# Retention's values and gate projected together by seven half-size products, in a single-core hybrid decoder block

## The chip, the core and the metric

The kernel runs on one core of a Trainium2 chip. A core has five engines with queues of their own, each worked through in order: TensorE (PE: matmuls, and PEld, its weight loads), VectorE (DVE), ScalarE (ACT), GpSimd (POOL) and SyncE (SP, which here only issues DMAs). The metric is device time in microseconds (us), the median of several executions; less is better.

## The reference

One decoder layer on 512 tokens of 1024 features, float32. What matters here is its front:

```python
h = rmsnorm(x, g_mix[l])
z = h @ w_in[l]
q_r, k_r, v_r, gt_r, q_f, k_f, v_f, f_f, a_r, a_f = split_cols(z)
q_r = rotary(...); k_r = rotary(...) * (RET_DK ** -0.5)
o_r = retention_chunkwise(q_r, k_r, v_r)        # 4 heads, values of 128, chunks of 128
...                                             # group norm of o_r
y_r = (silu(gt_r) * o_r) @ w_ret_o[l]
...                                             # forgetting attention of q_f, k_f, v_f: 8 heads of 64
x = x + (sigmoid(a_r) * y_r + sigmoid(a_f) * y_f) @ w_out[l]
x = x + swiglu(rmsnorm(x, g_ffn[l]))
```

v_r (values) and gt_r (gate) have 512 columns each and stand side by side in w_in: together a product of 512 x 1024 by 1024 x 1024. The norm's factor 1/rms of each token (rstd1) is applied after the products, since it is one number per token.

## The kernel before

Every float32 factor is split in a high and a low part (xh, xl of x times g_mix; wh, wl of weights), and a product is three matmuls: high by high, low by high, high by low (`three`). A weight unit is 128 x 1024 (0.5 MB): `load_w` issues its DMA on SP into one of two raw tiles, `split_raw` makes wh on ACT (a cast, L152) and wl on DVE (a subtraction, L153) in one of three pairs of tiles (WB = 3), used in turn. A pair is written again when PE has done with it, a raw tile when wl is made.

The order of the work: first the columns of retention's q and k (8 feature blocks by 4 token blocks, 96 matmuls into PSUM banks sc and tp), with loads and splits of x and weights running just ahead. Beside it x comes again, token by token; ACT squares and sums it (L220) and DVE makes rstd1 by a shift and three Newton steps (`rsqrt`, 12 instructions on 128x4). ACT then copies the four banks to rz, times rstd1.

Then the values: `tok_group`, 96 matmuls with 512 columns into the four acc banks, each copied by ACT to vr times rstd1. Then a stretch whose PE order is written out by hand (`pinned`): retention for four token blocks (rotation on POOL, `ret_rotate`; transposes, scores, states, norm, output) and the attention (`fox_scores`, `fox_turn`, `fox_values`, a chain of 32 steps), with a filling between their parts. `Fill` holds generators of independent matmuls and gives out so many us of them, by a cost of its own, at each call: the gate (group 4, with silu), the attention's q, k and v, and two of four pairs of gate tiles (`gates(mp)`, the columns a_r and a_f). RF, CF, PF and SF are the shares given out at each place; `fill.until(n)` empties all but n generators. Behind the attention the rest of the block follows: the third and fourth pair of gate tiles with the output projections, w_out, and the feed-forward part, which already computes its products by seven half-size products each.

Elsewhere the order on an engine is a scheduler's: it places instructions by its own estimate of when they are ready, and `after(a, b)` keeps a behind b.

Of the kernel before, what the change touches and what calls it, by code (L numbers as in the profile page):

```python
# [17 lines left out]
P = 128  # L18
# [34 lines left out]
@with_exitstack  # L53
def block_kernel(ctx: ExitStack, tc, x, xT, c_early, c_tab, c_late, w_qf, w_tok, w_a, w_y, w_o, w_gu, w_dn, w_dh, out):
    nc = tc.nc
# [53 lines left out]
    def rsqrt(dst, ss, inv_n, shape, nm, pool=None, behind=None):  # L109

        v = (pool or sm).tile(shape, F32, name=nm + "v", tag=nm + "v", bufs=1 if pool else 2)
        yi = (pool or sm).tile(shape, I32, name=nm + "y", tag=nm + "y", bufs=1 if pool else 2)
        a = (pool or sm).tile(shape, F32, name=nm + "a", tag=nm + "a", bufs=1 if pool else 2)
        y = yi.bitcast(F32)
        first = ts(out=v, in0=ss, scalar1=inv_n, scalar2=EPS, op0=ALU.mult, op1=ALU.add)
        if behind is not None:
            after(first, behind)
        ts(out=yi, in0=v.bitcast(I32), scalar1=1, scalar2=None, op0=ALU.logical_shift_right)
        ts(out=yi, in0=yi, scalar1=-1.0, scalar2=float(0x5F3759DF), op0=ALU.mult, op1=ALU.add)
        for i in range(3):  # L120
            stt(out=a, in0=y, scalar=-0.5, in1=y, op0=ALU.mult, op1=ALU.mult)
            tt(out=a, in0=a, in1=v, op=ALU.mult)
            stt(out=dst if i == 2 else y, in0=a, scalar=1.5, in1=y, op0=ALU.add, op1=ALU.mult)

# [23 lines left out]
    def split_raw(raw, width=1024):  # L148
        pool, bufs = next_pool(part_pools, 1)
        h = pool.tile([P, WP if pool is wp else 1024], F32R, name="wh", tag="wh", bufs=bufs)  # L150
        l = pool.tile([P, WP if pool is wp else 1024], F32R, name="wl", tag="wl", bufs=bufs)
        nc.scalar.copy(out=h[:, :width], in_=raw[:, :width])  # L152
        tt(out=l[:, :width], in0=raw[:, :width], in1=f32(h)[:, :width], op=ALU.subtract)  # L153
        return h, l
# [59 lines left out]
    pinned[0] = False  # L214
    ahead = [load_w(w_tok[3, u]) for u in range(2)]
    for t2 in range(2):
        nc.sync.dma_start(out=xs[t2], in_=x[t2 * 256:(t2 + 1) * 256].rearrange("(t p) d -> p t d", p=P))
    for t in range(NT):
        junk = ftok.tile([P, D], BF16, name="junk", tag="sq", bufs=1)
        act(out=junk, in_=xs[t // 2][:, t % 2, :], func=AF.Square, accum_out=ss1[:, t:t + 1])  # L220
    rsqrt(rstd1, ss1, 1.0 / D, [P, NT], "n1")
    nc.sync.dma_start(out=ctab, in_=c_tab)

# [75 lines left out]
    for t in range(NT):
        evac_to(rz, AF.Copy)(t, 0, accs[t])  # L300

    def unit(group):
        return lambda u, width: w_tok[group, u]

    run(tok_group(unit(3), evac_to(vr, AF.Copy), ahead=ahead))
    broadcast_cols(rstd1, r1)
# [12 lines left out]
    def ret_rotate(t):  # L319
# [138 lines left out]
    def fox_prep(a, part):  # L458

        if part == 0:  # L460
# [5 lines left out]
            for e, (r, o) in enumerate(((ra, rb), (rb, ra))):  # L466
                act(out=tk[e][r], in_=pk[r], func=AF.Copy, scale=gk[r])  # L467
                act(out=tk[e][o], in_=pk[r], func=AF.Copy, scale=gk[r])  # L468
                stt(out=kl[e][r], in0=pk[r], scalar=gk[r], in1=f32(tk[e])[r], op0=ALU.mult, op1=ALU.subtract)  # L469
            fox["k", a] = tk, kl  # L470
        else:
# [107 lines left out]
    fill.until(3)  # L579
    rwk.release()  # L580
# [69 lines left out]
    for mp in range(4):  # L650
        if mp > 0:
            if mp == 1:
                fill.until(0)
            else:
# [4 lines left out]
        for m2 in range(2):  # L659
# [346 lines left out]
def _layout(i):  # L1006
# [18 lines left out]
    def halves(m):  # L1025
# [42 lines left out]
```

## Time and profile before

| | us |
|---|---|
| median of 3 runs (715.22 to 717.8) | 716.05 |
| profiled execution, device time | 717.38 |
| its span, first to last instruction | 715.6 |
| PE busy | 708.9 |
| DVE busy | 509.2 |
| ACT busy | 344.0 |
| POOL busy | 70.1 |

A row of a group names line, engine, operation, what it writes and reads, shapes and count; then busy us, mean ns of one; then the engine's idle time just ahead of it and what ended it. A row of the timeline begins with start and length in us. A row of busy time by stage gives the stretch, its length, then for PE, PEld, DVE, ACT and POOL the busy time and in brackets the number of instructions, then the granted clock, the DMA engines' share and GB/s. A row of the chain has start, length, and the instructions merged.

### The profile page before, as it was taken

Reading aid. Unit: us, or ns where it says so; the run is one execution under the profiler, and the core shown is the slowest. Engines: PE = TensorE matmul, PEld = TensorE weight load, DVE = VectorE, ACT = ScalarE, POOL = GpSimd, SP = SyncE. Lnnn points to the kernel's source line nnn. Section 1 sums busy time; section 2 is a strip of 40 time slices with the busy share of each in tenths; the row PEclk is TensorE's granted clock in tenths of the full one; section 3 lists DMA queues with packets and bytes.
Section 4 is the critical chain, followed back from the end, with each engine's and each line's share of the span. In section 5 each row is a group of like instructions: output and inputs, shape, how many; then the busy total and the mean of one; then the engine's idle time right before and its main releaser. Section 6 shows DMA issues by size and latency. Waiting matters only on the chain.

```text
span 715.6 us, 10855 instructions
## 1 busy us (share of the span) xinstructions
PE 708.9 (99%) x4307; PEld 623.7 (87%) x4307; DVE 509.2 (71%) x844; ACT 344.0 (48%) x532; POOL 70.1 (10%) x90
## 2 busy tenths in 40 slices
PE   8999999999999999999999999999999999999998
PEld 6888998888777688888888999999999998888998
DVE  6333667756878673545968798899888998854684
ACT  4542434446766732233654755655665555533251
POOL 0163502121311100000220000000000000000000
PEclk9999999999999999999999999999999999999999
DMA  8632222233212023326603233322332213353112
GB/s 286 248 118 90 63 87 62 87 121 119 96 65 73 31 89 101 105 89 220 221 1 117 69 110 119 118 71 106 120 118 92 86 56 122 120 173 99 56 69 75
DMA packets 19908, 76.34 MB, mean 107 GB/s; under 512 B 2312, under 2 KB 2952, under 8 KB 16656
## 3 DMA queue, kind: packets, MB, share of 16 engines
q1 hardware_dynamic: 19712, 75.62, 31.2%
q8 instruction: 34, 0.56, 0.3%
q14 instruction: 18, 0.15, 0.1%
q10 hardware_dynamic: 144, 0.02, 0.0%
HBM read 73.52 MB, written 2.11 MB: 106 GB/s over the span
## 4 chain that ended last, share of the span: by engine, by line
PE 92%; DVE 3%; ACT 2%; issue 1%; POOL 1%; DMA 1%; SPq 0%; DVEq 0%; ACTq 0%
PE acc L72 59%; PE sc L72 27%; PE tp L72 5%; PE tp L75 2%; DVE pr L499 1%; POOL cb L491 1%; DVE pr L503 1%; DMA raw<-in_w_tok_dram 1%; ACT pr L501 1%; ACT tk L468 0%; DVE tq L478 0%; ACT tk L467 0%; DVE kl L469 0%; DVE sg L548 0%; DVE ofl L172 0%
## 5 line engine op out<-in xcount | busy, mean ns | idle before, releaser
L152 ACT CAST wh<-raw 128x1024 fp32r<-128x1024 f32 (+1 forms) x52 | 54.5, 1050 | 123.4 <-PE acc L72 97.4
L153 DVE TENSOR_TENSOR wl<-raw,wh 128x1024 fp32r<-128x1024 f32 (+1 forms) x52 | 66.6, 1282 | 48.4 <-ACT wh L152 48.3
L72 PE MATMUL sc<-xfh,cl 128*128 128x256 f32 x288 | 83.2, 289 | 0.0
L72 PE MATMUL sc<-xfh,ch 128*128 128x256 f32 x288 | 81.6, 283 | 0.0
L72 PE MATMUL sc<-xfl,ch 128*128 128x256 f32 x288 | 81.4, 283 | 0.0
L72 PE MATMUL acc<-wh,xh 128*128 128x512 f32 (+2 forms) x192 | 69.7, 363 | 0.0
L741 DVE TENSOR_TENSOR cl<-t,ch 128x1024 fp32r<-128x1024 f32 x48 | 58.6, 1222 | 13.7 <-ACT ch L741 13.6
L72 PE MATMUL acc<-wh,xl 128*128 128x512 f32 (+2 forms) x192 | 68.2, 355 | 0.0
L72 PE MATMUL acc<-wl,xh 128*128 128x512 f32 (+2 forms) x192 | 68.0, 354 | 0.0
L72 PE MATMUL acc<-xfh,ah 128*128 128x256 f32 (+1 forms) x216 | 63.9, 296 | 0.0
L72 PE MATMUL acc<-xfh,al 128*128 128x256 f32 (+1 forms) x216 | 63.7, 295 | 0.0
L72 PE MATMUL acc<-xfl,ah 128*128 128x256 f32 (+1 forms) x216 | 63.7, 295 | 0.0
L741 ACT CAST ch<-t 128x1024 fp32r<-128x1024 f32 x48 | 50.5, 1052 | 12.8 <-PE tp L72 8.0
L72 PEld LDWEIGHTS sc<-xfh,cl 128*128 128x128 f32 x288 | 55.0, 191 | 0.8 <-DVE cl L741 0.2
L72 PEld LDWEIGHTS sc<-xfh,ch 128*128 128x128 f32 x288 | 55.1, 191 | 0.1
L72 PEld LDWEIGHTS sc<-xfl,ch 128*128 128x128 f32 x288 | 55.1, 191 | 0.0
L72 PE MATMUL acc<-xh,wh 128*128 128x512 f32 x128 | 51.8, 404 | 0.0
L72 PE MATMUL acc<-xh,wl 128*128 128x512 f32 x128 | 50.0, 391 | 0.0
L72 PE MATMUL acc<-xl,wh 128*128 128x512 f32 x128 | 49.9, 390 | 0.0
L741 DVE TENSOR_TENSOR al<-raw,ah 128x1536 fp32r<-128x1536 f32 x24 | 42.2, 1757 | 6.9 <-ACT ah L741 6.9
L72 PEld LDWEIGHTS acc<-xfh,al 128*128 128x128 f32 x216 | 41.3, 191 | 1.0
L72 PEld LDWEIGHTS acc<-xfl,ah 128*128 128x128 f32 x216 | 41.3, 191 | 0.9
(294 smaller groups left out, 1796.3 us busy)
## 6 DMA issues: line engine op xcount, KB each, us to landing
raw<-in_w_gu_dram SPq DMA_DIRECT2D x21, 1024.0 KB, 4.8
raw<-in_w_tok_dram SPq DMA_DIRECT2D x16, 512.0 KB, 3.7
raw<-in_w_a_dram SPq DMA_DIRECT2D x16, 512.0 KB, 3.6
t<-in_w_dn_dram SPq DMA_DIRECT2D x14, 512.0 KB, 3.7
raw<-in_w_y_dram SPq DMA_DIRECT2D x8, 512.0 KB, 3.6
raw<-in_w_o_dram SPq DMA_DIRECT2D x8, 512.0 KB, 3.7
raw<-in_w_dh_dram SPq DMA_DIRECT2D x4, 1024.0 KB, 4.8
xf<-in_xT_dram SPq DMA_DIRECT2D x8, 256.0 KB, 5.0
```

The source lines that it names most:

```text
L72: in_order(nc.tensor.matmul(o, **kw))
L75: in_order(nc.tensor.transpose(out=o, in_=src, identity=ident))
L152: nc.scalar.copy(out=h[:, :width], in_=raw[:, :width])
L153: tt(out=l[:, :width], in0=raw[:, :width], in1=f32(h)[:, :width], op=ALU.subtract)
L491: gp.tensor_tensor(out=cb[:, qs], in0=cb[:, qs], in1=mask, op=ALU.add)
L499: nc.vector.tensor_tensor_reduce(out=pr[:, :n], in0=cb[:, :n], in1=sc[:, :n], scale=-1.0, scalar=3e38, op0=ALU.add, op1=ALU.min, accum_out=nm)
L501: fox["last"] = act(out=pr[:, :n], in_=pr[:, :n], func=AF.Exp, scale=-1.0, bias=nm, accum_out=rs)
L503: ts(out=pr[:, :n], in0=pr[:, :n], scalar1=ri, scalar2=None, op0=ALU.mult)
L741: split_to.last = nc.scalar.copy(out=h, in_=src), tt(out=l, in0=src, in1=f32(h), op=ALU.subtract)
```

## The change

Values and gate are computed as one product by a scheme with seven half-size products in place of eight. x's transposed blocks are paired: even and odd feature blocks are the two halves of the inner dimension, the first and second 256 tokens those of the rows, so A11, A12, A21, A22; the weights are four blocks B11 (even, values), B12 (even, gate), B21, B22 (odd), each 512 x 512 and loaded as a tile of two halves (blk1, blk0, blk2, blk3 in this order). With S1 = A21 - A22, S2 = S1 - A11, S3 = A11 - A21, S4 = S2 + A12 and T1 = B11 + B12, T2 = T1 + B22, T3 = B12 + B22, T4 = T2 + B21, the products are, in program order: A11 B11 into the banks x_; S1 T1 into z_; S2 T2 added to x_; A12 B21 into y_ (banks sc); S3 T3 added to x_; S4 B22 added to z_; A22 T4 added to x_. Each has 4 feature pairs x 2 token blocks x 3 = 24 matmuls with 512 columns. The running sums in x_ are needed between the products, so ACT copies x_, times rstd1, to u before the next product is added; DVE combines u, y_ and z_ to vr and gs.

x in the tile xf is now scaled by g_mix in place (ACT, 8 instructions), since the sums need it. Each sum is split like a weight (`x_sum`: sh on ACT, sl on DVE). rsqrt is put behind the low part of T1, the Square instructions behind its cast. The gate's group leaves the filling and the third pair of gate tiles joins it; the shares SF get smaller, and each product of the attention's values gets a share VF ahead of it and stands ahead of the next transposes. Some buffer counts change (SG 8 to 12, PT and CBUF 3 to 2), POOL's first rotation is put behind the low part of T3, and in `fox_prep` two DVE instructions stand behind the ACT ones.

```diff
-    RAW, WB, SG, PT, PR, TB, CBUF = 2, 3, 8, 3, 4, 2, 3
+    RAW, WB, SG, PT, PR, TB, CBUF = 2, 3, 12, 2, 4, 2, 2
-    RF, CF, PF, SF, LAG = (5.32, 4.64, 5.6, 4.6, 11.2), (3.0, 2.0, 2.26, 4.0), 5.9, (0.83, 1.03, 1.77, 1.6), 3
+    RF, CF, PF, SF, LAG = (5.32, 4.64, 5.6, 4.6, 11.2), (3.0, 2.0, 2.26, 4.0), 5.9, (0.63, 0.83, 1.57, 1.4), 3
+    VF = 1.8
...
-    ahead = [load_w(w_tok[3, u]) for u in range(2)]
+    load_block(1)
+    load_block(0)
     for t2 in range(2):
         nc.sync.dma_start(out=xs[t2], in_=x[t2 * 256:(t2 + 1) * 256].rearrange("(t p) d -> p t d", p=P))
-    for t in range(NT):
-        junk = ftok.tile([P, D], BF16, name="junk", tag="sq", bufs=1)
-        act(out=junk, in_=xs[t // 2][:, t % 2, :], func=AF.Square, accum_out=ss1[:, t:t + 1])
-    rsqrt(rstd1, ss1, 1.0 / D, [P, NT], "n1")
+    load_block(3)
+    load_block(2)
+    for k in range(NK):
+        xk = xf[k // 4][:, k % 4, :]
+        act(out=xk, in_=xk, func=AF.Copy, scale=gmix(k))
...
-    run(tok_group(unit(3), evac_to(vr, AF.Copy), ahead=ahead))
+    def x_sum(n, p, q, op, behind=None):
+        for i in range(2):
+            to = sums[:, n, 2 * i:2 * i + 2, :]
+            p_, q_ = (to if b is None else xv[i][:, :, b[0], b[1]:b[1] + HS] for b in (p, q))
+            one = tt(out=to, in0=p_, in1=q_, op=op)
+            if behind is not None:
+                after(one, behind)
+        h = bp.tile([P, 4, HS], F32R, name="sh", tag="sh", bufs=2)
+        l = bp.tile([P, 4, HS], F32R, name="sl", tag="sl", bufs=2)
+        split_to_parts(sums[:, n], h, l)
+        return lambda j, tp: tuple(f[:, j, tp * P:(tp + 1) * P] for f in (h, l))
...
+    def halves_of(block, add=None, behind=None):
+        parts = []
+        for v in range(2):
+            if add is not None:
+                one = tt(out=block[:, v, :], in0=block[:, v, :], in1=add[:, v, :], op=ALU.add)
+                if behind is not None:
+                    after(one, behind)
+            parts.append(split_raw(block[:, v, :]))
+        return parts
...
+    def products(os, parts, stat, new, by_bank=False):
+        steps = [(j, tp) for j in range(4) for tp in range(2)]
+        for j, tp in sorted(steps, key=lambda s: s[1]) if by_bank else steps:
+            h, l = parts[j // 2]
+            cs = slice(j % 2 * 512, j % 2 * 512 + 512)
+            sh, sl = stat(j, tp)
+            for n, (a, b) in enumerate(((sh, h), (sl, h), (sh, l))):
+                mm(os[tp], lhsT=a, rhs=b[:, cs], start=new and j + n == 0, stop=j == 3 and n == 2, skip_group_check=not new)
+
+    def scaled(o, bank_, t):
+        act(out=o, in_=bank_, func=AF.Copy, scale=rstd1[:, t:t + 1])
...
+    b11 = halves_of(B11)
+    products(x_, b11, x_block(A11), True)
+    s1, t1 = x_sum(0, A21, A22, ALU.subtract), halves_of(B11, B12, split_raw.last[1])
+    for t in range(NT):
+        junk = ftok.tile([P, D], BF16, name="junk", tag="sq", bufs=1)
+        after(act(out=junk, in_=xs[t // 2][:, t % 2, :], func=AF.Square, accum_out=ss1[:, t:t + 1]), split_raw.last[0])
+    t1_low = split_raw.last[1]
+    r_last = rsqrt(rstd1, ss1, 1.0 / D, [P, NT], "n1", behind=t1_low)
+    us = [ftok.tile([P, 4, 512], F32, name="u", tag=n) for n in ("qf", "kf")]
+    for tp in range(2):
+        scaled(us[tp][:, 0, :], x_[tp], tp)
+    for t in range(NT):
+        evac_to(rz, AF.Copy)(t, 0, accs[t])
+    products(z_, t1, s1, True)
+    for tp in range(2):
+        scaled(us[tp][:, 3, :], z_[tp], tp + 2)
+    s2 = x_sum(0, None, A11, ALU.subtract)
+    products(x_, halves_of(B11, B22), s2, False)
...
+    products(x_, halves_of(B11, B21, r_last), x_block(A22), False, by_bank=True)
+    for tp in range(2):
+        scaled(vr[:, tp + 2, :], x_[tp], tp + 2)
...
-    fill = Fill(tok_group(unit(4), evac_to(gs, AF.Silu)), tok_group(lambda u, width: w_qf[u, :, :width], evac_qf, (256, 264)),
-                tok_group(unit(1), evac_kf), tok_group(unit(0), evac_to(vf, AF.Copy)), gates(0), gates(1))
+    fill = Fill(tok_group(lambda u, width: w_qf[u, :, :width], evac_qf, (256, 264)),
+                tok_group(unit(1), evac_kf), tok_group(unit(0), evac_to(vf, AF.Copy)), gates(0), gates(1), gates(2))
```

What it does to the queues, at three places. In the rows a name's number tells tiles apart; blk1 holds B11 and then T1, T2 and T4, blk0 B12 and then T3; sums and sh, sl belong to the sums of x, n1 and rstd1 to rsqrt.

DVE, where rstd1 is made; before:

```order
L153 TENSOR_TENSOR wl_332<-raw_286,wh_331 128x1024 [waits DMAHW1_49,Activation_49]
L153 TENSOR_TENSOR wl_360<-raw_288,wh_359 128x1024 [waits DMAHW2_49,Activation_49]
L115 TENSOR_SCALAR n1v_300<-ss1_85 128x4 [waits Activation_49]
L118 TENSOR_SCALAR n1y_301<-n1v_300 128x4 [waits DVE_49]
L119 TENSOR_SCALAR n1y_301<-n1y_301 128x4 [waits DVE_49]
```

The twelve steps stood in a row behind two low parts. The same place now:

```order
L118 TENSOR_SCALAR n1y_376<-n1v_375 128x4 [waits DVE_49]
L155 TENSOR_TENSOR wl_437<-blk1_287,wh_436 128x1024 [waits PE_49,Activation_49]
L119 TENSOR_SCALAR n1y_376<-n1y_376 128x4 [waits DVE_49]
L343 TENSOR_TENSOR blk0_286<-blk0_286,blk3_289 128x1024
L121 SCALAR_TENSOR_TENSOR n1a_377<-n1y_376 128x4 [waits DVE_49]
L155 TENSOR_TENSOR wl_469<-blk2_288,wh_468 128x1024 [waits DMAHW1_49,PE_49,Activation_49]
L122 TENSOR_TENSOR n1a_377<-n1a_377,n1v_375 128x4 [waits DVE_49]
L333 TENSOR_TENSOR sl_503<-sums_314,sh_502 128x1024 [waits Activation_49]
L123 SCALAR_TENSOR_TENSOR n1y_376<-n1a_377,n1y_376 128x4 [waits DVE_49]
```

They stand behind all of T1 and the first half of T2, with the two sums of T3 (the first stands just ahead of these rows), the second low part of T2, that of B21 and that of S3 between them.

PE, where the second product ends and the third begins, now (before, its matmuls of the values went on here and only waited for their splits):

```order
L72 MATMUL acc_316<-wl_364,sh_353 128x512
L72 MATMUL acc_317<-wh_431,sh_426 128x512 [waits Activation_49]
L72 MATMUL acc_317<-wh_431,sl_427 128x512
L72 MATMUL acc_317<-wl_432,sh_426 128x512 [waits DVE_49]
L72 MATMUL acc_318<-wh_431,sh_426 128x512 [waits Activation_49]
```

acc_317 and acc_318 are x_, which PE may write again when ACT has copied each to u. These copies on ACT:

```order
L154 CAST wh_436<-blk1_287 128x1024 [waits DVE_49,PE_49]
L154 CAST wh_468<-blk2_288 128x1024 [waits DMAHW1_49,PE_49]
L332 CAST sh_502<-sums_314 128x1024 [waits DVE_49,PE_49]
L359 ACTIVATE u_390<-acc_317,rstd1_86 128x512 [waits DVE_49]
L359 ACTIVATE u_391<-acc_318,rstd1_86 128x512 [waits Activation_49]
L303 ACTIVATE rz_313<-sc_186,rstd1_86 128x512
```

They wait for DVE's rstd1, and the copies to rz, formerly the first to use it, stand behind them.

ACT, at the end of the values; before:

```order
L152 CAST wh_522<-raw_520 128x1024 [waits DMAHW2_49,DVE_49,PE_49]
L293 ACTIVATE vr_321<-acc_327,rstd1_86 128x512 [waits PE_49]
L293 ACTIVATE vr_321<-acc_328,rstd1_86 128x512 [waits PE_49]
L293 ACTIVATE vr_321<-acc_329,rstd1_86 128x512 [waits PE_49]
L293 ACTIVATE vr_321<-acc_330,rstd1_86 128x512 [waits PE_49]
L152 CAST wh_589<-raw_587 128x1024 [waits DMAHW3_49,DVE_49]
```

The copies that free the banks stood ahead of the next cast. Now (raw_674, raw_728 and raw_827 are the first three units of the attention's q):

```order
L154 CAST wh_676<-raw_674 128x1024 [waits DMAHW5_49,PE_49,Activation_49]
L402 ACTIVATE gs_549<-gs_549 128x512 [waits DVE_49] x2
L359 ACTIVATE vr_548<-acc_317,rstd1_86 128x512 [waits PE_49]
L154 CAST wh_730<-raw_728 128x1024 [waits DMAHW6_49,PE_49,Activation_49]
L154 CAST wh_829<-raw_827 128x1056 [waits DMAHW7_49,PE_49,Activation_49]
L359 ACTIVATE vr_548<-acc_318,rstd1_86 128x512 [waits PE_49]
```

The copy of acc_318 stands behind the cast of the third unit, which waits for a load (DMAHW7).

More of the change, by code (lines that the diff above doesn't have):

```diff
@@ L151, in split_raw @@
         l = pool.tile([P, WP if pool is wp else 1024], F32R, name="wl", tag="wl", bufs=bufs)
-        nc.scalar.copy(out=h[:, :width], in_=raw[:, :width])
-        tt(out=l[:, :width], in0=raw[:, :width], in1=f32(h)[:, :width], op=ALU.subtract)
+        split_raw.last = (nc.scalar.copy(out=h[:, :width], in_=raw[:, :width]),
+                          tt(out=l[:, :width], in0=raw[:, :width], in1=f32(h)[:, :width], op=ALU.subtract))
         return h, l
@@ L296, in block_kernel, with unit @@
     rz = rtok.tile([P, NT, 512], F32, name="rz", tag="rz")
+    def unit(group):
+        return lambda u, width: w_tok[group, u]
+    B12, B11, B21, B22 = blocks
+    xv = [f.rearrange("p (j o) t -> p j o t", o=2) for f in xf]
+    HS = S // 2
+    A11, A12, A21, A22 = ((0, 0), (1, 0), (0, HS), (1, HS))
+    sums = ftok.tile([P, 2, 4, HS], F32, name="sums", tag="vf")
+    def x_sum(n, p, q, op, behind=None):
[9 more added lines that the diff above has]
+        return lambda j, tp: tuple(f[:, j, tp * P:(tp + 1) * P] for f in (h, l))
@@ new lines, in split_to_parts, with x_block @@
+    def split_to_parts(src, h, l):
+        nc.scalar.copy(out=h, in_=src)
+        tt(out=l, in0=src, in1=f32(h), op=ALU.subtract)
+    def x_block(b):
+        return lambda j, tp: tuple(f[:, 2 * j + b[0], b[1] + tp * P:b[1] + (tp + 1) * P] for f in (xh, xl))
+    def halves_of(block, add=None, behind=None):
+        parts = []
+        for v in range(2):
+            if add is not None:
[4 more added lines that the diff above has]
+        return parts
@@ new lines, in scaled @@
+    def scaled(o, bank_, t):
+        act(out=o, in_=bank_, func=AF.Copy, scale=rstd1[:, t:t + 1])
+    z_ = [bank("acc") for _ in range(2)]
+    x_ = [bank("acc") for _ in range(2)]
+    pinned[0] = True
+    b11 = halves_of(B11)
[4 more added lines that the diff above has]
+        after(act(out=junk, in_=xs[t // 2][:, t % 2, :], func=AF.Square, accum_out=ss1[:, t:t + 1]), split_raw.last[0])
@@ L297, in block_kernel @@
+    for tp in range(2):
+        scaled(us[tp][:, 1, :], x_[tp], tp)
+    y_ = [bank("sc") for _ in range(2)]
+    products(y_, halves_of(B21), x_block(A12), True)
+    s3 = x_sum(1, A11, A21, ALU.subtract, t1_low)
+    t3 = halves_of(B12, B22, t1_low)
+    t3_low = split_raw.last[1]
+    products(x_, t3, s3, False)
+    for tp in range(2):
+        scaled(us[tp][:, 2, :], x_[tp], tp + 2)
+    s4 = x_sum(0, None, A12, ALU.add, r_last)
     vr = rtok.tile([P, NT, 512], F32, name="vr", tag="rtok0")
@@ L298, in block_kernel @@
     gs = rtok.tile([P, NT, 512], F32, name="gs", tag="rtok1")
[L299 to L303, printed above, removed]
-    run(tok_group(unit(3), evac_to(vr, AF.Copy), ahead=ahead))
+    for tp in range(2):
+        stt(out=vr[:, tp, :], in0=y_[tp], scalar=rstd1[:, tp:tp + 1], in1=us[tp][:, 0, :], op0=ALU.mult, op1=ALU.add)
+    products(z_, halves_of(B22), s4, False)
+    for tp in range(2):
+        tt(out=gs[:, tp + 2, :], in0=us[tp][:, 3, :], in1=us[tp][:, 2, :], op=ALU.subtract)
+        act(out=gs[:, tp + 2, :], in_=gs[:, tp + 2, :], func=AF.Silu)
+        stt(out=gs[:, tp, :], in0=z_[tp], scalar=rstd1[:, tp:tp + 1], in1=us[tp][:, 1, :], op0=ALU.mult, op1=ALU.subtract)
+        act(out=gs[:, tp, :], in_=gs[:, tp, :], func=AF.Silu)
@@ L306, in block_kernel @@
+    products(x_, halves_of(B11, B21, r_last), x_block(A22), False, by_bank=True)
+    for tp in range(2):
+        scaled(vr[:, tp + 2, :], x_[tp], tp + 2)
+    pinned[0] = False
+    bp.release()
+    orp = tc.alloc_tile_pool(name="orp", bufs=1, side="right")
+    sgp = tc.alloc_tile_pool(name="sgp", bufs=1, side="right")
     broadcast_cols(rstd1, r1)
@@ L327, in ret_rotate @@
         tb = rwk.tile([P, 2, RH, 32], F32, name="tb", tag="tb", bufs=1)
-        gp.tensor_tensor(out=ta, in0=z1, in1=c, op=ALU.mult)
+        first = gp.tensor_tensor(out=ta, in0=z1, in1=c, op=ALU.mult)
+        if t == 0:
+            tc.add_manual_dep(first.ins, t3_low.ins.name, mybir.DependencyInfo(mybir.DependencyClass.Sync, mybir.DependencyReason.DATA), reason="GpSimd's part comes behind most of the sums")
         gp.tensor_tensor(out=tb, in0=z2, in1=s, op=ALU.mult)
@@ L578, in block_kernel @@
     ret_out(NT - 1)
-    fill.until(3)
+    fill.until(4)
     rwk.release()
```

39 lines of the change are left out of this document (24 added, 15 removed).

## Prediction

> **What bounds the kernel now.** I read the page's head first, then the chain that ended last, then busy time by stage.
>
> ```profile
> span 715.6 us, 10855 instructions
> PE 708.9 (99%) x4307; PEld 623.7 (87%) x4307; DVE 509.2 (71%) x844; ACT 344.0 (48%) x532; POOL 70.1 (10%) x90
> PE 92%; DVE 3%; ACT 2%; issue 1%; POOL 1%; DMA 1%; SPq 0%; DVEq 0%; ACTq 0%
> ```
>
> TensorE (PE) has work for 708.9 of 715.6 us and is 92% of the chain. So a removed matmul is worth its whole slot, and a new wait of PE costs its whole length. Two rows of busy time by stage (the second column is the length, then PE):
>
> ```profile
> 30.10:52.00 21.90, 21.90 (x100) 18.11 (x99) 8.96 (x18) 8.80 (x14) 13.99 (x16) 1.00 0.30 96
> 169.00:248.00 79.00, 77.28 (x418) 58.90 (x417) 60.70 (x168) 54.48 (x126) 16.62 (x29) 1.00 0.22 71
> ```
>
> In the first, the projection of the values, PE has no idle time, while VectorE (DVE) works 8.96 us of 21.90 and ScalarE (ACT) 8.80. The second is the attention: PE idles 1.72 us of 79, the one place in mid-kernel where it waits at all. The chain gives the price of a 512-column matmul:
>
> ```profile
> 30.11 21.76 PE acc L72 x96
> ```
>
> 21.76 / 96 = 0.2267 us.
>
> **What is removed.** Values and gate are 2 x 96 such matmuls; seven products of 24 make 168. 24 x 0.2267 = **-5.44 us**, all of it on PE's path. Weights loaded stay 4 MB. The Square and rsqrt work stays too.
>
> **What is added, and where it lies.** DVE gets 8 half-sums of x (512 columns), 8 sums of weight halves (1024 columns), 4 splits of sums, and the last combinations. These rows price them; the last stretch of DVE is quoted because there an rsqrt stands between wide operations, as it will here:
>
> ```profile
> L750 DVE TENSOR_TENSOR t<-raw 128x1024 f32<-128x1024 f32 x24 | 29.3, 1219 | 0.1
> L755 DVE TENSOR_TENSOR t<-t,raw 128x512 f32<-128x512 f32 x24 | 16.5, 689 | 0.5
> 380.33 0.15 DVE L115 TENSOR_SCALAR n1v<-tp 128x4 f32<-128x4 f32 x1
> 380.44 0.69 DVE L755 TENSOR_TENSOR t<-t,raw 128x512 f32<-128x512 f32 x1
> 381.05 0.16 DVE L118 TENSOR_SCALAR n1y<-n1v 128x4 int32<-128x4 int32 x1
> 381.12 1.22 DVE L741 TENSOR_TENSOR cl<-t,ch 128x1024 fp32r<-128x1024 f32 x1
> 382.26 0.16 DVE L119 TENSOR_SCALAR n1y<-n1y 128x4 int32<-128x4 int32 x1
> 382.33 0.68 DVE L756 TENSOR_TENSOR t<-t,raw 128x512 f32<-128x512 f32 x1
> 387.50 0.16 DVE L122 TENSOR_TENSOR n1a<-n1a,n1v 128x4 f32<-128x4 f32 x1
> 387.69 0.16 DVE L123 SCALAR_TENSOR_TENSOR rstd<-n1a,n1y 128x4 f32<-128x4 f32 x1
> ```
>
> Start to start, a 1024-column operation takes 1.14 us (381.12 to 382.26), a 512-column one 0.61, a small rsqrt step 0.08 between wide ones and 0.20 behind another step.
>
> **The first new wait: PE for rstd1.** The third product (T2 x S2) is added into the banks x_ of the first, so both banks must first be copied to u. That copy multiplies by rstd1. Before, nothing on PE waited for rstd1: the four banks of the first projection were sc and tp, and the values went into acc. When is rstd1 ready now?
>
> ```profile
> 19.27 1.05 ACT L152 CAST wh<-raw 128x1024 fp32r<-128x1024 f32 x1 [2.36 <-PE tp L72]
> 24.71 1.05 ACT L152 CAST wh<-raw 128x1024 fp32r<-128x1024 f32 x1 [4.38 <-PE tp L72]
> 25.66 1.05 ACT L220 ACTIVATE junk<-xs 128x1024 bf16<-128x1024 f32 x1
> 26.84 1.06 ACT L220 ACTIVATE junk<-xs 128x1024 bf16<-128x1024 f32 x1
> 32.84 1.27 ACT L293 ACTIVATE rz<-sc,rstd 128x512 f32<-128x512 f32 x2 [2.48 <-DVE rstd L123]
> 32.58 0.16 DVE L123 SCALAR_TENSOR_TENSOR rstd<-n1a,n1y 128x4 f32<-128x4 f32 x1
> ```
>
> Now it is 32.7 us. After the change I follow the queues in their new order. There are three pairs of split buffers. The two halves of B11 take those released at 19.27 and 24.71; the first half of T1 needs the pair that PE reads until the first projection ends, at 30.3. Cast 1.05, so DVE starts its low part at 31.4. From there to the end of rsqrt DVE's queue holds eleven 1024-column operations (12.5 us), two of 512 (1.2), six interleaved small steps (0.5) and seven in a row (1.4): 15.7 us without a pause, so rstd1 at 47.1. ACT's squares don't shorten this: the first stands behind the cast of T1's second half, whose buffer is free at 33.0; four at 1.18 (25.66 to 26.84) and one cast put the last at 39.7, when DVE comes to the first step anyway. The copy of the first bank takes 0.69 and PE goes on at 48.0. It is done with the second product at 30.11 + 48 x 0.2267 = 41.0. **+7.0 us.** Lower end: a DVE with no pause from 19.4 (sixteen wide operations, six of 512, the steps: 23.8 us) gives rstd1 at 43.2 and a wait of 2.9. Upper end: every operation at its full duration instead of its spacing, +1.1, so 8.1. I take 7.0, since the buffer is the row nearest to it.
>
> What waits behind that copy on ACT: rz (rotations on POOL, not wanted by PE for 30 us), the copies of the second product, and the next cast. Worked on in the same way, the other halves come 1 to 4 us ahead of PE, so I cost them at nothing; their cover is PE's 5.44 us for each product.
>
> **The pace after the pause.** No row shows what PE does after 7 idle us in mid-kernel. The nearest is the start, where it comes from idleness:
>
> ```profile
> 6.89 1.05 PE L72 MATMUL tp<-wh,xh 128*128 128x512 f32 x2
> 7.75 1.05 PE L72 MATMUL sc<-wh,xl 128*128 128x512 f32 x2
> 10.31 0.74 PE L72 MATMUL tp<-wl,xh 128*128 128x512 f32 x2
> 10.88 0.63 PE L72 MATMUL sc<-wh,xh 128*128 128x512 f32 x2
> ...
> 206.28 0.66 PE L75 MATMUL tp<-ctab,pr 128*128 128x128 f32 x4 [0.30 <-ACT pT L518]
> 206.70 0.47 PE L72 MATMUL acc<-xh,wh 128*128 128x512 f32 x1
> 207.01 0.39 PE L72 MATMUL acc<-xl,wh 128*128 128x512 f32 x1
> ```
>
> A pair takes 0.86 us there, 0.43 each, until 10.7, and then 0.23, while the granted clock in the rows reads 1.00. Twelve f32 matmuls ran slowly: 12 x 0.20 = 2.4 us. The other end is 0, as after the short gaps of the attention. A gap of 7 us is nearer to the start: **+2.4**. The Trainium skill, TensorE: Matmul & The Clock Gate, section "What's actually happening", says that the array falls to half its clock after an idle window of about 3.4 us and needs about as long of work to leave it. An estimate by that page would be 1.7 us lost (half of 3.4) and a sum 0.7 lower; the trace agrees with the half pace at the start, and no run here shows the fall.
>
> **The second new wait: PE for a bank behind a load.** The next group (qf) reuses the banks of the sixth and seventh products. The copy of the last of these, vr for the fourth block of tokens, now stands on ACT behind the cast of qf's third unit. That unit's raw buffer (one of two) comes free only when the low part of qf's first unit is made, and that stands on DVE behind the gate's last combinations, which wait for the sixth product.
>
> ```profile
> raw<-in_w_qf_dram SPq DMA_DIRECT2D x2, 528.0 KB, 3.5
> L196 DVE SCALAR_TENSOR_TENSOR xl<-xf,ce,xh 128x512 fp32r<-128x512 f32 x8 | 6.0, 748 | 0.8 <-ACT xh L194 0.8
> L152 ACT CAST wh<-raw 128x1056 fp32r<-128x1056 f32 x2 | 2.1, 1070 | 6.4 <-PE acc L72 6.4
> L293 ACT ACTIVATE vr<-acc,rstd 128x512 f32<-128x512 f32 x4 | 2.7, 689 | 2.3 <-PE acc L72 2.3
> 42.52 1.52 DVE L153 TENSOR_TENSOR wl<-raw,wh 128x1024 fp32r<-128x1024 f32 x1 [3.07 <-ACT wh L152]
> 47.56 1.76 DVE L153 TENSOR_TENSOR wl<-raw,wh 128x1024 fp32r<-128x1024 f32 x1 [3.52 <-ACT wh L152]
> ```
>
> From the end of the sixth product: 1.2 until DVE is through the last low part of T4, two combinations 1.4, low part 1.2, load 3.5, cast 1.07, copy 0.69: 9.1 us. PE meanwhile has the seventh product (5.44), nine matmuls of 256 columns and two transposes (1.3): 6.7. **+2.3 us.** Ends: 0.8 if DVE is early by one wide operation and one combination; 3.6 where POOL's rotations run beside it (1.52 and 1.76 instead of 1.23).
>
> **The third pair of gate tiles in the filling.** The gate's group left the filling (20.5 us by its own cost), the third pair entered (20.5). So it lasts as long as before, and the attention's shares (0.63 + 0.83 + 1.57 + 1.4 for four steps, and 1.8 before each product of values) sum to the old ones. The bias gets two buffers instead of three, so one comes free a head earlier than its load is wanted.
>
> ```profile
> cb<-cd SPq DMA_DIRECT2D x8, 256.0 KB, 3.5
> L194 ACT ACTIVATE xh<-xf,ce 128x512 fp32r<-128x512 f32 x8 | 5.8, 723 | 8.5 <-DMA xf<-in_xT_dram 6.6 <-DMA ce<-in_c_early_dram 1.9
> 20.00:30.10 10.10, 10.10 (x46) 8.38 (x45) 2.45 (x2) 5.62 (x9) 0.00 (x0) 1.00 0.91 352
> ```
>
> A bias load takes 3.5 us and a head some 9 (79 us for eight and their lead), so it is hidden. Ends: -1.7 (all of PE's idling there goes) and +3.5 (one load late). I take 0.
>
> At the front, eight ACT scalings of xT (0.72 each) lie in the 8.5 us in which ACT waits for loads. In SP's queue the four blocks (4.2 MB) go around x (2.1 MB) and ahead of the tables. At 352 GB/s from about 16 us, where the first projection's loads end, two blocks and x are there at 28, the block that T2 needs a half at a time at 31 (its first half at 29.5, wanted at 33.7), all blocks at 34 and the tables at 37 (wanted by POOL after 48). Both cost 0; their cover is 4 us or more.
>
> **The sum.** -5.44 + 7.0 + 2.4 + 2.3 = +6.3. The profiled execution took 717.38 us (span 715.6), which gives 723.7; it lies 1.33 over the median of 716.05. Against the median: **722.3 us**.
>
> **Rivals.** A measurement of this kernel can tell about 0.5% (3.6 us) from no change.
>
> - *Both waits, but PE keeps its pace after the pause* (or the attention loses its idling instead): 716.05 + 3.9 = 720.0. For it: the granted clock reads 1.00 throughout. Against it: so it does in the slow first 10.7 us. Beside this: the Trainium skill's page on the clock gate speaks against this case, since 7 us is two of its windows.
> - *Only the wait for rstd1, without a slow restart; the bank comes in time*: 716.05 - 5.4 + 7.0 = 717.7, no change. It needs the load or DVE 2.3 us earlier than I have it.
> - *Faster: PE never waits*, 716.05 - 5.4 = 710.6. The place is rstd1: the copy must be done at 41.0, so rstd1 written by 40.3, 6.8 us earlier than I find. DVE has 15.7 us of work from 31.4 on and would have to do it in 8.9; that decides only where its eleven wide operations start 0.52 us apart. For it: DVE works less than half of this stage now, so there seems to be room. Against it: the 1.14 us spacing, and a buffer that PE holds until 30.3.
> - *Heavier*: the second wait reaches 3.6 us and PE restarts slowly again (+1.3, +2.4), or one bias load is late in the attention (+3.5): about 726.
> - *The change doesn't do what it says*: the products replace 192 matmuls by 168 in the program, and the filling keeps its length; no time hangs on this.
>
> **Chances.** The sum as it stands 0.48 (720.8 to 724.5, if each term is off by its likely error); PE keeps its pace 0.22; only the first wait 0.12; faster 0.07; heavier 0.11. The range leaves out the faster case and the far half of the heavier one, and goes to the edge of the third: 716.0 to 726.0. Slower by over 0.5% (above 719.6): 0.47 + 0.12 + 0.11 = 0.70. Within it: 0.01 + 0.10 + 0.12 = 0.23. Faster: 0.07.
>
> **What would show it.** In the new trace: PE's acc row with an idle of about 7 us before the 49th matmul behind the first projection, ended by ACT's copy to u; the next ten or twelve matmuls 0.43 us apart; ACT's copy waiting for DVE's rstd; another idle of about 2 us of PE soon after the first 256-column matmuls, ended by ACT's vr; and 24 matmuls fewer at 0.2267. I am wrong if rstd1 is written near 41, if the first matmuls after the pause are 0.23 apart, or if the load of qf's third unit starts before the seventh product does.

## The result, and the profile after

The changed kernel takes 722.94 us (median of 6 runs, 721.64 to 724.15) against 715.99 (6 runs, 715.22 to 717.8): a ratio of 1.0095, 95% interval 1.0079 to 1.0111. The change costs about 7 us.

The head of the page after, and the chain's shares:

```profile
span 720.4 us, 10869 instructions
PE 703.4 (98%) x4283; PEld 618.4 (86%) x4283; DVE 541.6 (75%) x876; ACT 363.5 (50%) x556; POOL 75.1 (10%) x90
PE 88%; DVE 5%; ACT 3%; issue 2%; POOL 1%; DMA 1%; SPq 0%; ACTq 0%; DVEq 0%
```

The 24 matmuls are gone (4307 to 4283) and PE is busy for 5.5 us less. That this is 24 x 0.2267 is chance, as the stretches below show. The span grew all the same: DVE has 32 us more work, and the chain leaves PE for DVE and ACT oftener. PE idles 17 us of the span where it idled 6.7.

The two profiled executions must not be subtracted as they are, since they differ at the start, where PE has the same work in both. The timeline of PE, first of before, then of after: the first matmul behind the first projection, and the first of the feed-forward products.

```profile
29.95 0.39 PE L72 MATMUL acc<-wh,xh 128*128 128x512 f32 x1
...
395.05 0.28 PE L72 MATMUL sc<-xfh,ch 128*128 128x256 f32 x1
```

```profile
6.48 0.63 PE L72 MATMUL tp<-wh,xh 128*128 128x512 f32 x2
...
27.82 0.39 PE L72 MATMUL acc<-wh,xh 128*128 128x512 f32 x1
...
399.73 0.28 PE L72 MATMUL sc<-xfh,ch 128*128 128x256 f32 x1
```

In after the first matmuls ran 0.23 us apart (a pair from 6.48) where before's took 0.43 until 10.7, so it came to the changed part 2.1 us sooner. From mark to mark before takes 365.10 us and after 371.91: **+6.81**, near the 6.95 between the medians, and behind the second mark both take 320.6. I use this length, called the middle stretch, for every kernel below. In it PE is busy for 363.34 us before and 360.21 after: 3.1 less, since matmuls at half pace count as busy for longer. The other 2.4 us of the 5.5 are the quicker start.

Where the 6.81 arose. PE at the third product (idle time and its ender in brackets), then the copy on ACT and the factor on DVE:

```profile
38.48 0.39 PE L72 MATMUL acc<-wl,sh 128*128 128x512 f32 x1
45.49 0.80 PE L72 MATMUL acc<-wh,sh 128*128 128x512 f32 x1 [6.62 <-ACT u L359]
46.08 0.63 PE L72 MATMUL acc<-wh,sl 128*128 128x512 f32 x1
...
48.64 0.58 PE L72 MATMUL acc<-wh,sl 128*128 128x512 f32 x1
49.05 0.40 PE L72 MATMUL acc<-wl,sh 128*128 128x512 f32 x1
...
52.71 0.39 PE L72 MATMUL sc<-wh,xh 128*128 128x512 f32 x1
```

```profile
29.25 1.22 DVE L155 TENSOR_TENSOR wl<-blk,wh 128x1024 fp32r<-128x1024 f32 x1
...
37.34 0.16 DVE L115 TENSOR_SCALAR n1v<-ss 128x4 f32<-128x4 f32 x1
...
44.55 0.16 DVE L123 SCALAR_TENSOR_TENSOR rstd<-n1a,n1y 128x4 f32<-128x4 f32 x1
44.75 1.27 ACT L359 ACTIVATE u<-acc,rstd 128x512 f32<-128x512 f32 x2 [4.08 <-DVE rstd L123]
```

PE's second product was through at 38.71 and the third began at 45.49, released by the copy to u, which waited for rstd1: **+6.8**. The third product then took 52.71 - 45.49 = 7.22 us instead of 5.44: **+1.8**. Unlike at the start, the granted clock (third number from the right) shows why. Rows: a stretch, its length, busy time of PE, PEld, DVE, ACT, POOL, clock, DMA share, GB/s.

```profile
38.90:42.00 3.10, 0.00 (x0) 0.00 (x0) 3.10 (x5) 1.77 (x2) 0.00 (x0) 1.00 0.00 0
42.00:43.00 1.00, 0.00 (x0) 0.00 (x0) 1.00 (x3) 0.00 (x0) 0.00 (x0) 0.60 0.00 0
45.50:48.90 3.40, 3.40 (x8) 2.72 (x9) 3.40 (x5) 3.40 (x7) 0.97 (x1) 0.50 0.00 0
49.00:50.00 1.00, 1.00 (x6) 0.77 (x5) 0.12 (x1) 0.53 (x2) 0.00 (x0) 0.99 0.00 0
```

A mean of 0.60 between 42 and 43 puts the fall to one half at 42.2, 3.5 us into the pause; 0.99 between 49 and 50 puts the return at 49.0. The first eight matmuls ran at half pace. The second wait comes behind the seventh product. PE's row of the waits, then DVE and ACT:

```profile
PE tp L75 <- DVE rb L248: 2.0, 2, 1.1
```

```profile
75.41 2.51 DVE L248 TENSOR_SCALAR rb<-ones,rstd 128x128 f32<-128x128 f32 x2
76.08 1.07 ACT L154 CAST wh<-raw 128x1056 fp32r<-128x1056 f32 x1 [1.90 <-DMA raw<-in_w_qf_dram]
77.05 0.68 ACT L359 ACTIVATE vr<-acc,rstd 128x512 f32<-128x512 f32 x1
```

**+2.0**, but ended by the tiles rb that PE turns (77.92), with the copy of vr's bank 0.2 us ahead of them (77.73). Last, the attention, first of before, then of after:

```profile
100.00:120.00 20.00, 19.96 (x128) 17.31 (x127) 16.01 (x58) 10.59 (x17) 2.50 (x3) 1.00 0.25 80
160.00:260.00 100.00, 98.28 (x513) 76.21 (x512) 73.77 (x186) 64.21 (x138) 18.00 (x32) 1.00 0.25 80
```

```profile
100.00:120.00 20.00, 19.24 (x114) 16.07 (x113) 17.22 (x59) 11.02 (x17) 8.15 (x8) 1.00 0.27 80
200.00:280.00 80.00, 77.64 (x417) 58.35 (x416) 60.54 (x164) 56.95 (x127) 16.36 (x28) 1.00 0.21 66
```

PE idles 0.76 + 2.36 there instead of 0.04 + 1.72: **+1.4**. The ledger: -5.44 + 6.8 + 1.8 + 2.0 + 1.4 = +6.6, of 6.81.

### The profile page after: what moved, and what is told of

Its sections match the earlier page's. It is cut to its first block, busy times and chain, and to the rows that moved or that the text cites. A ratio compares the mean times of both kernels' runs of the same rounds, so it can differ in the third digit from the quotient of the medians.

```text
span 720.4 us, 10869 instructions
## 1 busy us (share of the span) xinstructions
PE 703.4 (98%) x4283; PEld 618.4 (86%) x4283; DVE 541.6 (75%) x876; ACT 363.5 (50%) x556; POOL 75.1 (10%) x90
## 3 DMA queue, kind: packets, MB, share of 16 engines
HBM read 73.52 MB, written 2.11 MB: 105 GB/s over the span
## 4 chain that ended last, share of the span: by engine, by line
PE 88%; DVE 5%; ACT 3%; issue 2%; POOL 1%; DMA 1%; SPq 0%; ACTq 0%; DVEq 0%
PE acc L72 55%; PE sc L72 27%; PE tp L72 5%; PE tp L75 1%; DVE pr L607 1%; DVE wl L155 1%; POOL cb L599 1%; ACT wh L154 1%; ACT pr L609 1%; ACT tk L574 1%; DMA raw<-in_w_tok_dram 1%; ACT tk L573 1%; DVE kl L576 1%; DVE pr L611 0%; ACT tq L584 0%
## 5 line engine op out<-in xcount | busy, mean ns | idle before, releaser
L154 ACT CAST wh<-raw 128x1024 fp32r<-128x1024 f32 (+1 forms) x44 | 46.2, 1050 | 93.9 <-PE acc L72 84.7
L72 PE MATMUL sc<-xfh,ch 128*128 128x256 f32 x288 | 81.6, 283 | 0.0
L155 DVE TENSOR_TENSOR wl<-raw,wh 128x1024 fp32r<-128x1024 f32 (+1 forms) x44 | 56.3, 1280 | 26.1 <-ACT wh L154 26.1
L72 PE MATMUL acc<-wh,xh 128*128 128x512 f32 (+2 forms) x144 | 50.5, 351 | 0.8 <-DVE mv L502 0.8
L72 PE MATMUL acc<-wl,xh 128*128 128x512 f32 (+2 forms) x144 | 49.4, 343 | 0.0
L72 PE MATMUL acc<-wh,xl 128*128 128x512 f32 (+2 forms) x144 | 49.4, 343 | 0.0
L848 DVE TENSOR_TENSOR al<-raw,ah 128x1536 fp32r<-128x1536 f32 x24 | 42.2, 1757 | 6.9 <-ACT ah L848 6.9
```

The source lines that it names most:

```text
L72: in_order(nc.tensor.matmul(o, **kw))
L154: split_raw.last = (nc.scalar.copy(out=h[:, :width], in_=raw[:, :width]), tt(out=l[:, :width], in0=raw[:, :width], in1=f32(h)[:, :width], ...
L848: split_to.last = nc.scalar.copy(out=h, in_=src), tt(out=l, in0=src, in1=f32(h), op=ALU.subtract)
```

## The experiments

All kernels below start from the changed kernel. Their ratios are to before.

**rstd1 in a row.** DVE's queue alone is changed:

```diff
-    products(x_, halves_of(B11, B22), s2, False)
+    products(x_, halves_of(B11, B22, low=(1, r_last)), s2, False)   # low part behind rstd1
-    products(y_, halves_of(B21), x_block(A12), True)
+    products(y_, halves_of(B21, low=(0, r_last)), x_block(A12), True)
...   # and the sums of T3, the low part of S3
```

> The copies stay scaled, but the twelve small instructions of rstd1 run in a row, and what DVE had between them (three lows, two sums) stands behind them. Theory A: rstd1 at 39.8 in place of 44.55 us of the profile after, the bank free at 40.6, so PE waits 1.9 us in place of 6.8; after so short a wait I expect no slow restart (-1.8); 722.9 - 4.9 - 1.8 = 716.2, within 0.3% of before. Rival B (DVE is the bound, the lows put back are now late): a wait of 2 to 4 us appears at the third or the fifth product, 718 to 720.

717.26 us (12 runs), ratio 1.0011 (0.9999 to 1.0023); middle stretch 367.15, so -4.8 against after. DVE and PE, then PE's clock at the second wait:

```profile
36.97 0.17 DVE L115 TENSOR_SCALAR n1v<-ss 128x4 f32<-128x4 f32 x1
39.15 0.16 DVE L123 SCALAR_TENSOR_TENSOR rstd<-n1a,n1y 128x4 f32<-128x4 f32 x1
40.20 0.50 PE L72 MATMUL acc<-wh,sh 128*128 128x512 f32 x1 [1.50 <-ACT u L363]
```

```profile
69.50:72.70 3.20, 1.68 (x10) 1.29 (x11) 2.28 (x3) 2.14 (x3) 3.20 (x5) 1.00 0.55 174
73.00:76.00 3.00, 3.00 (x16) 3.00 (x15) 0.34 (x1) 0.00 (x0) 3.00 (x3) 0.50 0.49 168
```

Theory A holds for the first wait: twelve steps take 2.3 us in place of 7.4 (37.34 to 44.71 in after), PE waits 1.5 and starts at full pace, and rival B's wait at the third or fifth product did not come. The time is 1.1 us above A's 716.2, since some came back: the second wait's three short stops (0.59, 0.35 and 0.91 between 69.2 and 71.9) were followed by 3.4 us of half clock with PE busy throughout, some sixteen matmuls of 256 columns 0.21 us apart in place of 0.12.

**First copies unscaled.** rstd1 is taken off the banks altogether, and its instructions put later:

```diff
-        scaled(us[tp][:, 0, :], x_[tp], tp)
+        kept(us[tp][:, 0, :], x_[tp])           # plain copy; likewise z_, x_ and rz
...
+    r_last = rsqrt(rstd1, ss1, 1.0 / D, [P, NT], "n1", behind=t3_low)
+    for t in range(NT):
+        scaled(rz[:, t, :], rz[:, t, :], t)
```

> The copies of the first product (and of the three later ones, and of rz) leave their banks unscaled; rstd1 is multiplied in later, off the banks, and is made behind the parts of the fifth product. Theory A (PE waits for rstd1 and for nothing else): the wait of 6.8 us ahead of the third product goes, and the slow restart of 1.8 us with it; the second wait of 2.0 us stays, since its chain (third raw buffer, rb) hangs on the last product; 722.9 - 8.6 = 714.3, that is 0.2% faster than before. Rival B (the third product's own parts are late too, with DVE the true bound): PE waits at the next link, for wl of the second or of the fifth product, 2 to 5 us, and the time stays at 716 to 719. Rival C (the time is lost in attention or elsewhere, not here): it stays above 720.

725.42 us (4 runs), ratio 1.0124 (1.0108 to 1.0139); middle stretch 375.06, 3.2 longer than after's. PE from the third product to the fifth, then at the sixth, and what held it there:

```profile
39.00:57.00 18.00, 18.00 (x81) 14.79 (x79) 15.33 (x26) 11.72 (x16) 0.00 (x0) 1.00 0.01 2
```

```profile
60.83 0.58 PE L72 MATMUL acc<-wh,sh 128*128 128x512 f32 x1 [3.58 <-ACT sh L332]
64.80 0.79 PE L72 MATMUL acc<-wh,sl 128*128 128x512 f32 x1 [3.39 <-DVE sl L333]
56.20 1.28 DVE L323 TENSOR_TENSOR sums<-sums,xf 128x512 f32<-128x512 f32 x2
56.32 2.56 ACT L359 ACTIVATE rz<-rz,rstd 128x512 f32<-128x512 f32 x4 [0.88 <-DVE rstd L123]
59.73 1.05 ACT L332 CAST sh<-sums 128x1024 fp32r<-128x1024 f32 x1
```

The first wait and the slow restart are gone, as A says: no idle time from 39 to 57. But the sums of S4 stand behind rstd1 by the kernel's own order (`r_last`), and I had moved rstd1 behind the fifth product's parts. The sixth product then waited 7.0 us in two pieces with the clock falling between them, and the second wait grew to 2.9 us (1.96 and 0.90), with half clock behind it. None of the three theories had this, though C's time (above 720) came: the wait was moved, not taken away.

**Both waits at once, on that version:** this edit with the two on the second wait that are shown below.

> The edit of the unscaled copies together with both edits on the second wait: rstd1 is spread by one wide copy and turned ahead of the last product, and the copy of vr's third tile stands ahead of the cast of qf's third unit. Theory A: first wait (6.8), slow restart (1.8) and second wait (2.0) all go, 722.9 - 10.6 = 712.3, 0.5% faster than before. Rival B (DVE or ACT is the next bound, since both have to do the same work in 10 us less): PE waits 2 to 5 us in smaller pieces, and the time is 714 to 718.

723.45 us (6 runs), ratio 1.0094 (1.008 to 1.0108), with the same two stops at the sixth product, 3.6 and 4.3 us. Both forecasts (712.3, and 714 to 718) missed for the reason that the run before shows; the second wait was absent.

**Zeros in the pause.** 24 matmuls of a zero tile, added to z_:

```diff
     products(z_, t1, s1, True)
+    for _ in range(24):
+        mm(z_[0], lhsT=warm[:, 0:P], rhs=warm, start=False, stop=True, skip_group_check=True)
```

> Nothing is taken from the wait: 24 matmuls of zeros, added to a bank that is not read yet, run between the second product and the third, 24 x 0.227 = 5.4 us inside the 6.6 us of idle time. Theory D (the half pace of the first matmuls of the third product comes from PE having stood still): with 1.2 us of idle time left all 24 matmuls of the third product run 0.227 us apart, 5.4 us in place of 7.2, and the time falls by 1.8 us to 721.1. Rival E (they are slow because of what stands beside them, the copies of the banks or the loads): the third product still takes about 7.2 us and the time stays at 722.9. If PE is not fed in time behind the zeros, it is longer.

722.98 us (6 runs), ratio 1.0082 (1.0067 to 1.0097); middle stretch 370.61, -1.3.

```profile
39.18 5.13 PE L72 MATMUL acc<-warm 128*128 128x512 bf16 x23
45.80 0.50 PE L72 MATMUL acc<-wh,sh 128*128 128x512 f32 x1 [1.49 <-ACT u L359]
```

```profile
42.70:45.40 2.70, 1.61 (x8) 0.53 (x6) 2.49 (x9) 0.34 (x1) 0.00 (x0) 1.00 0.00 0
45.50:48.90 3.40, 3.10 (x13) 2.55 (x14) 3.40 (x4) 3.40 (x7) 0.97 (x1) 1.00 0.00 0
```

The wait ends where it did, and the clock stays at 1.00: the third product's matmuls run 0.227 apart from the second on. So it was PE's standing still, not the copies beside it (D, not E). The gain of 1.3 to 1.6 us shows in the trace; in 6 runs the medians can't tell it from nothing.

**The second wait, each chain alone.** One run each:

```diff
+    broadcast_cols(rstd1, r1, ftok.tile([P, NT, P], F32, name="wide", tag="sq", bufs=1))  # one wide copy, four turns
     products(x_, halves_of(B11, B21, r_last), x_block(A22), False, by_bank=True)
...
-    broadcast_cols(rstd1, r1)
```

> The four tiles of rstd1 that are turned behind the last product (rb) are made by one wide copy right behind rstd1 and turned ahead of the last product; the copy of vr's bank stays behind the cast of qf's third unit. Prediction's theory F (the copy of vr's bank ends the second wait): PE still waits about 2 us there, now for ACT vr. Rival G (the turns of rb end it, as the trace of after names them; the bank is free 0.25 us earlier): PE goes into the filling at once and stops only where its fourth bank is needed, 0.7 to 0.9 us in place of 2.0. First wait and slow restart as in after.

```diff
-        scaled(vr[:, tp + 2, :], x_[tp], tp + 2)
+        split_raw.hold = split_raw.count + 3, scaled(vr[:, tp + 2, :], x_[tp], tp + 2)   # the cast of qf's third unit behind it
```

> The other half: the copy of vr's fourth tile is put ahead of the cast of qf's third unit on ACT, so that it no longer stands behind a load; rb is left as it is. Theory F: PE's second wait falls from 2.0 to under 0.5 us. Rival G: it stays at 1.9 to 2.2 us and ends on DVE rb, as before.

And both edits:

> Both halves at once. By F and by G alike the second wait goes to under 0.4 us: 722.9 - 1.8 = 721.1, ratio to before 1.007. If something third is late there (the low part of qf's second unit, which DVE makes 1.7 us behind its cast), 0.5 to 1.5 us of it stay, 721.6 to 722.6.

PE's waits between 24 and 90 us, in this order; of the third this is the only one:

```profile
PE acc L72 <- ACT vr L359: 1.7, 1, 1.7
```

```profile
PE tp L75 <- DVE rb L253: 2.0, 2, 1.1
```

```profile
PE acc L72 <- ACT u L364: 6.4, 1, 6.4
```

Each alone gains next to nothing (722.83 and 723.29 us in one run each; middle stretches 372.42 and 371.61): the other chain ends the wait at nearly the same time. In the first run (rb alone) the stop in one piece also cost the clock, which the 2.0 us in two pieces had not: 1.5 us after it PE's matmuls fell from 0.12 to 0.21 us apart, for 3.4 us.

```profile
77.74 0.39 PE L72 MATMUL acc<-wh,xh 128*128 128x256 f32 x1 [1.73 <-ACT vr L359]
...
79.50 0.42 PE L72 MATMUL acc<-wl,xh 128*128 128x256 f32 x1
79.71 0.41 PE L72 MATMUL acc<-wh,xl 128*128 128x256 f32 x1
```

Both together remove the wait: 719.88 us (5 runs), ratio 1.0049 (1.0035 to 1.0062), middle stretch 369.40, -2.5. So F was right that the bank's copy costs about 2 us, and G that rb does; neither was the cause alone, and my guess of a wait under 0.9 with rb out of the way was wrong.

**A version to keep the gain.** rstd1 in a row, the first product's two copies alone unscaled (u is multiplied later, in place), and both edits on the second wait:

> A version meant to keep the 24 matmuls saved and to lose both waits: rstd1 in a row (as in the run with the row), the two copies of the first product alone unscaled (multiplied by rstd1 later, in place), rb by one wide copy and turned early, vr's copy ahead of the cast. From the run with the row, 717.3: its wait of 1.5 for ACT u goes, and its second wait of 1.8 goes; 714.0, 0.35% faster than before. Rival B (DVE, which in the run with the row stood idle nowhere between 32 and 67 us, is now the bound of this stretch): PE gets 1 to 2 us of waits for wl and sl instead, and the time is 715 to 716.

715.94 us (11 runs), ratio 0.9998 (0.9987 to 1.0009). The rival was right: DVE and ACT are late with the seventh product's second part, 1.61 us, where ACT's cast had itself waited for DVE's sum of T4. With 0.29 just before it, half clock followed here too. PE, ACT, then the stretches:

```profile
64.78 0.80 PE L72 MATMUL acc<-wh,xh 128*128 128x512 f32 x1 [1.61 <-ACT wh L155]
63.68 1.04 ACT L155 CAST wh<-blk 128x1024 fp32r<-128x1024 f32 x1 [2.02 <-DVE blk L350]
```

```profile
61.30:64.70 3.40, 1.59 (x6) 0.67 (x4) 3.40 (x4) 1.38 (x3) 3.24 (x3) 1.00 0.00 0
64.90:68.00 3.10, 3.00 (x7) 1.90 (x8) 2.81 (x2) 2.30 (x4) 3.02 (x3) 0.50 0.00 0
```

**The gates behind the last product's parts.** On that version:

```diff
+    products(x_, halves_of(B11, B21, r_last), x_block(A22), False, by_bank=True)
+    parts_last = split_raw.last[1]
     for tp in range(2):
-        tt(out=gs[:, tp + 2, :], ...)
+        after(tt(out=gs[:, tp + 2, :], ...), parts_last)
...
-    products(x_, halves_of(B11, B21, r_last), x_block(A22), False, by_bank=True)
```

> The version before it (rstd1 in a row, first copies unscaled, both halves of the second wait's edits) lost 1.9 us ahead of and in the last product, whose parts stood behind the gates' subtractions and Silu on DVE and ACT, and then ran 8 matmuls at half pace. Here the gates stand behind those parts. If that was the cause, PE waits there under 0.7 us, keeps its pace, and the time falls by 1.2 + 1.6 us from 715.9 to 713.1, 0.5% faster than before. Rival: the gates are late next (their banks are the first that the filling needs), PE waits 1 to 2 us at the filling's start, and it is 714.5 to 716.

713.99 us (7 runs), ratio **0.9963 (0.9952 to 0.9975)**: faster than before by 2.6 us and than the changed kernel by 9. Its page, the one wait of PE left between 24 and 90 us, and the products:

```profile
PE 703.4 (99%) x4283; PEld 618.3 (87%) x4283; DVE 540.2 (76%) x873; ACT 363.8 (51%) x558; POOL 78.8 (11%) x90
```

```profile
PE acc L72 <- ACT vr L368: 0.4, 1, 0.4
38.90:66.00 27.10, 27.10 (x122) 22.12 (x121) 26.54 (x35) 21.68 (x30) 13.77 (x10) 1.00 0.00 1
```

PE is busy without a gap while DVE works 26.54 of 27.10 us: in these products the two are now level. The middle stretch is 362.21, 2.9 under before; -5.44 + 0.4 and the attention's +1.4 give -3.6, so 0.7 us of loss is left. It is PE's busy time, 358.62 us of the stretch against 363.34: 4.7 less and not 5.44. Where it arose stays open. The same with the last product by halves:

> As the run beside it, but the last product goes by halves of its operand in place of by bank, so its second part is needed 1.4 us later and both its banks end together. If the second part is late there: no wait in the product, 0.3 to 0.5 us less than the run beside it. If vr's two copies, now one behind the other, are what the filling waits for: 0.5 to 0.7 us more.

713.44 us (7 runs), ratio 0.9961 (0.9948 to 0.9974), middle stretch 362.25: no difference that these runs can tell. Two short waits, 0.45 for DVE's wl and 0.20 for ACT's vr, stand in place of the one of 0.41.

**The attention's orders.** Two edits undone in the changed kernel, one run each:

```diff
-            for e, r in enumerate((ra, rb)):        # run "kl": subtractions between the copies again
...
-            fox_values(v // 8)                       # run "turn": values behind the turn again
```

> The changed kernel with one edit of the attention undone: a pair's values stand behind the turn of the same step again, as before the change. PE's idle time in the attention (200 to 280 us) is 2.36 us in after and was 1.69 in before (160 to 260). If that order makes the new idle time, it falls to 1.7; if it came with the smaller fillings or with fewer buffers for pT and cb, it stays at 2.3 or grows.

> The changed kernel with another edit of the attention undone: each subtraction (kl, and tq's other rows) stands between the copies of its pair again. The trace of after has one wait of 0.4 us for kl. If the order of these makes it, the wait goes; if not, it stays at 0.4. Effect on the time at most 0.5 us either way.

PE between 200 and 280 us, the run "turn", then the run "kl":

```profile
200.00:280.00 80.00, 77.89 (x418) 58.32 (x417) 60.68 (x165) 56.06 (x127) 16.63 (x29) 1.00 0.22 70
```

```profile
200.00:280.00 80.00, 77.40 (x418) 58.50 (x417) 60.41 (x165) 54.94 (x127) 16.34 (x29) 1.00 0.22 70
```

2.11 and 2.60 us idle, against 2.36; middle stretches 371.86 and 371.75 against 371.91. Without its order the wait for kl grew from 0.4 to 1.5 us, and another shrank. So neither order makes more than 0.3 us of the new idle time, by one run each. Whether the two buffers fewer (pT, cb) or the smaller fillings make it stays open: no run gave either back.

## Why the prediction was right

It forecast 722.3 and slower; measured 722.94. Step by step:

- *Removed, -5.44*: right in the 24 matmuls. The 5.5 us less of PE's busy time are no proof of the size, since they hold the quicker start and the slow matmuls. In the run with the gates behind the parts, where PE keeps its pace, PE is busy for 4.7 us less.
- *The first wait, +7.0*: right in place, cause and size: 6.8, ended by the copy to u behind rstd1, which was through at 44.71. The forecast's 47.1 counts from a start that was 2.1 us later in the execution it came from; so it is 0.3 us off. DVE worked without a pause from the low part of T1's first half (29.25) to there, 15.5 us for the 15.7 forecast, which had counted thirteen small steps for twelve. The two runs on rstd1 cut the wait to 1.5 us and to nothing. "Wanted 1 to 4 us ahead" held for the other products' parts as long as PE waited for rstd1; the unscaled runs showed how thin that cover is.
- *The pace after the pause, +2.4*: right in kind, oversized: +1.8 (eight slow matmuls, not twelve). The run with zeros shows the cause. The rival "PE keeps its pace" argued from a granted clock of 1.00 in the slow start; in mid-kernel the row did show 0.50, so the start's rows were no evidence. The Trainium skill, TensorE: Matmul & The Clock Gate, section "What's actually happening", has a free-running window of about 3.4 us after which an idle array is halved; the estimate of 1.7 by it came nearer than mine. The traces agree with the window's length: worked out as above from stretches of one us, half clock lasted 6.8 us here and at the sixth product with the unscaled copies, and 3.4 behind the shorter stops of four runs. That section asks for an idle window, though; with rstd1 in a row, 1.68 busy us of 3.20 were followed by half clock.
- *The second wait, +2.3*: right in place and size (2.0), half right in cause. The chain I followed (load, cast, copy of vr's bank) ended at 77.73 as derived, 8.7 us behind the sixth product in place of 9.1; but I took rb for ready, and it stood on DVE behind the low part of qf's second unit and ended 0.2 us later. The line "ended by ACT's vr" was thus wrong, and undoing that chain alone gained nothing.
- *The filling and the attention, 0*: the term that was mis-sized most: +1.4, within its ends (-1.7 and +3.5). Its reason, that the bias load is hidden, held; but PE's short waits for turned tiles and for a norm on DVE grew.
- The errors (-0.2, -0.6, -0.3, +1.4) cancel to 0.3: the sum is better than its terms, and that it came within 0.7 us is in part luck.

The case "faster", 710.6 where PE never waits, was rightly put on rstd1 as the point that decides; the best version here gets 3 us short of it.

## What to carry to other kernels

Fewer matmuls pay only if what replaces them keeps clear of PE: ask of each product which bank it is added to, who must copy that bank first, and what scalar the copy needs. A small chain of instructions put between wide ones on an in-order queue pays a wide one at each step (7.4 us in place of 2.3); where PE waits for its end, run it in a row, or take the factor off the bank. When a wait is undone, look for the chain that ends just behind it, and count short stops together, since in two runs here half clock followed them as it followed the long pause.

## What was not expected of the hardware

Short stops of PE were followed by half the granted clock as the pause of 6.6 us was: 0.59 + 0.35 + 0.91 us within 2.7, 0.29 + 1.61 within 3.1, 1.96 + 0.90 with the unscaled copies, and 1.73 in one piece with rb alone. A stop of 1.5 us was not, nor were the 2.0 us of the changed kernel's second wait (1.07 and 0.90). A fit, not shown: count on from the last return to full clock in steps of 3.41 us (half of the 6.82 from 42.20 to 49.02). With rb alone and with the unscaled copies the next fall (79.3 and 81.6) then comes nine and four steps behind the return (48.5 and 67.9). The changed kernel's second wait lies 0.6 us in one step and 1.4 in the next, and the 1.73 us lie in one. So an idle share of somewhere near half a step would be what it takes.

The profiled executions come to the end of the first projection at 27.5 to 28.2 us or at 29.4 to 30.0, by the pace of PE's first matmuls. The changed kernel (27.82) and the two runs that differ from it in the attention alone (29.49 and 29.38) fall on both sides: 2 us that belong to no edit.

The two small multiplications for rb on DVE, 0.24 us each at 48.65, took 1.25 each at 75.41, beside POOL.
